# Projections 2 and 3 ahead of the attention, the norm as a column, the rotation from raw projections, positions first

## The chip, the cores and the metric

One core of a Trainium2 chip. The metric is the device time of one execution in microseconds; the lower the better. The engines are called as in the profile: PE (TensorE; PEld is its weight load), DVE (VectorE), ACT (ScalarE), POOL (GpSimd) and SP (SyncE, which issues DMAs here).

## The reference

512 tokens of width 1024 pass through two blocks of two layers each. The change touches the first block alone. One of its layers:

```python
h = _rmsnorm(x, g_pre_mix[l])
z = h @ w_in[l]
zf, zq, zk, zv, zm = jnp.split(z, splits, axis=-1)
y_f = _fourier_mix(zf, w_fourier[l])
q = _rope(zq.reshape(b, s, N_Q_HEADS, HEAD_DIM), positions)
k = _rope(zk.reshape(b, s, N_KV_HEADS, HEAD_DIM), positions)
y_a = _window_attn(q, k, v, sink[l])
mkv = _rmsnorm(mem, g_mem[l]) @ w_mem_kv[l]
km, vm = jnp.split(mkv, 2, axis=-1)
y_m = _memory_attn(zm.reshape(b, s, N_MEM_HEADS, HEAD_DIM), km, vm)
y = jnp.concatenate([_rmsnorm(y_f, ..), _rmsnorm(y_a, ..), _rmsnorm(y_m, ..)], axis=-1) @ w_out[l]
x = x + _rmsnorm(y, g_post_mix[l])
h = _rmsnorm(x, g_pre_ffn[l])
gate, up = jnp.split(h @ w_ffn_in[l], 2, axis=-1)
x = x + _rmsnorm((jax.nn.silu(gate) * up) @ w_ffn_out[l], g_post_ffn[l])
```

`_rmsnorm` multiplies by a gain and by one number per token, 1/sqrt(mean of squares + eps). `_rope` rotates each head by an angle from the token's position, half of the head against the other half. The window attention sees 128 tokens to either side; the memory attention sees 256 memory tokens, the same in both layers.

## The kernel before

Activations lie with the features on the partitions and the 512 tokens along the row, so x is 8 tiles of 128x512. Every product is done to nearly float32 accuracy as three matmuls (`mm3`): each factor is split into a rounded high half and the low half that is left (`split`, `split_gain`), and high x low, low x high and high x high are added up. A weight tile of 256 KB is loaded twice by POOL's DMA queue (`halves`): once as the high half, then ScalarE or VectorE negates that, and a second DMA adds the weight to it, which leaves the low half. A projection of 128 features is 8 x 3 = 24 matmuls.

The gain of a norm is put into the split of x. The factor per token commutes with the projections, so it is multiplied onto them behind PSUM: `enter` (838) makes the halves and the sum of the squares of x, and `late` makes the factor `rb` as a tile of 128x512 by `wide` (817): two matmuls with ones, then mean, square root, reciprocal and one Newton step, all 512 wide. The other form, used elsewhere, is `inv` (801) with `bcast` (856): matmuls against one column of ones put the sums into 4 columns, POOL takes the power -1/2 of 128x4, VectorE multiplies that onto an identity, and one matmul against ones spreads it over the partitions.

A layer of the first block, `block1` (1190), has ten projections of `a_in`: 0 to 3 are the queries (a pair of heads each), 4 the keys, 5 the values, 6 and 7 the memory's queries, 8 and 9 the Fourier branch. Projections 4, 0, 5 and 1 come first: in layer 0 by `open`, which takes the weights as they arrive and waits with the norm, in layer 1 by `linear`, in halves of 256 columns. `ev` (1195) then takes each out of PSUM, times `rb`; for 0 to 4 it rotates (four SP DMAs swap the halves of the heads, times `sin1`, plus the other times `cos1`), and splits. The rotation tables come from `positions` and `trig`, called in `body` (921) behind the loads of x.

Then four pairs of window heads and two pairs of memory heads follow, two pairs ahead: `ask` (scores, softmax), `answer` (transposes), `put` (product with the values). Between these, `pull` takes matmuls from the generator `fillers` (1236), to keep PE busy: projections 2, 3 and 6, in layer 0 the memory's norm and its keys and values (`mem_in`, `mem_k`, `mem_v`; each of the two splits the 8 memory tiles of 128x256 anew), then 7, 8, 9 and the Fourier products. Each `yield` gives a cost in us as the program reckons it: 0.68 for three matmuls of a projection (5.44 for a projection), 0.7 for each of twelve Fourier steps (8.4). In layer 1 the pulls ask for 2 x 5.4 + 12 x 1.3 + 4 x 3.3 = 39.6. The norms of the three groups, the output projection `a_out` and the feed-forward part follow. Layer 1's memory keys and values lie beside layer 0's feed-forward part.

None of this is issued in the order written. `Plan` records every operation; `schedule` (425) then gives each engine its queue: PE's in the order recorded, every other operation by its `need`, the earliest PE time that depends on it by estimated costs, and many of them to the engine that is free. So every instruction of the profile has one line, 646 (649 in the changed kernel), and its names are those of tiles: `s` is one of 100 SBUF tiles of 2 KB per partition, `ps` one of 8 PSUM banks, `in_...` a tensor in memory, `ones`, `onesr`, `ident`, `nhalf` and `cols` constants, `rms` and `rinv` the columns of a norm.

## Time and profile before

| | |
|---|---|
| median of 3 runs | 3483.54 us (3479.14 to 3483.74) |
| profiled execution | 3481.36 us, its span 3479.6 us |
| granted PE clock, mean | 0.992 |
| PE busy | 3404.2 us (98%), 16296 matmuls |
| PEld, DVE, ACT, POOL busy | 2844.1 (82%), 1923.0 (55%), 893.1 (26%), 1748.9 (50%) |
| DMA | 635.93 MB, mean 183 GB/s |
| chain that ended last | PE 90%, DVE 4%, DMA 2%, the rest 4% |

A busy share is that of the whole span. The timeline of an engine lists runs of like instructions with their start, their duration and, in brackets, the idle time ahead of them and what ended it. The table of windows sums, for a stretch of the span, each engine's busy time and its instructions; the granted clock is a share of full speed.

### The profile page before, as it was taken

The numbers are of one execution on the slowest core, as the hardware profiler recorded it, in microseconds if no ns is written. First come the engines' busy times: TensorE is split into PE (matmuls) and PEld (weight loads), VectorE is DVE, ScalarE is ACT, GpSimd is POOL, SyncE is SP. The second block draws the span as 40 slices with busy tenths as digits, with TensorE's granted clock in tenths as the row PEclk, the third lists the DMA queues.
The fourth block names the chain that finished last, engine by engine and source line by source line (L and its number), as shares of the span: only waits on it lengthen the run. The fifth ranks groups of instructions, "written<-read, shape, count | busy, mean of one in ns | idle before, by whom it ended". The sixth has DMA issues, their size and how long they took to land.

```text
span 3479.6 us, 44666 instructions
## 1 busy us (share of the span) xinstructions
PE 3404.2 (98%) x16296; PEld 2844.1 (82%) x16296; DVE 1923.0 (55%) x3916; ACT 893.1 (26%) x1732; POOL 1748.9 (50%) x2433
## 2 busy tenths in 40 slices
PE   6999999899999999999999999999999999999998
PEld 4788888778888988888888888888888888888887
DVE  7964433876432733259997534244423999744332
ACT  5741002543000301016723200010001573411000
POOL 2455464364446544653456544664465336654462
PEclk8999999999999999999999999999999999999999
DMA  6688897798789887985899977998799669998794
GB/s 174 145 186 184 164 207 148 156 193 183 153 169 208 207 181 157 239 212 103 172 197 249 220 152 158 220 204 200 150 225 219 130 130 222 230 239 160 158 202 104
DMA packets 360444, 635.93 MB, mean 183 GB/s; under 512 B 40608, under 2 KB 63904, under 8 KB 360224
## 3 DMA queue, kind: packets, MB, share of 16 engines
q0 software_dynamic: 346752, 612.56, 82.4%
q1 hardware_dynamic: 13472, 20.52, 1.9%
q8 instruction: 128, 2.10, 0.2%
q14 instruction: 92, 0.75, 0.1%
HBM read 624.00 MB, written 6.29 MB: 181 GB/s over the span
## 4 chain that ended last, share of the span: by engine, by line
PE 90%; DVE 4%; DMA 2%; issue 1%; ACT 1%; POOL 1%; SPq 0%; POOLq 0%; DVEq 0%; ACTq 0%
PE ps L646 90%; DVE s L646 4%; ACT s L646 1%; DMA s<-in_x 1%; POOL s L646 0%; DMA s<-in_b_in 0%; DMA s<-in_pos 0%; DMA s<-in_a_in 0%; DMA s<-s 0%; POOL rinv L646 0%; DVE mx L646 0%; DMA s<-in_a_out 0%; DMA s<-in_a_mk 0%; SPq L646 0%; DVE sp L646 0%
## 5 line engine op out<-in xcount | busy, mean ns | idle before, releaser
L646 PE MATMUL ps<-s 128*128 128x512 f32 (+2 forms) x15706 | 3350.9, 376 | 44.6 <-DVE s L646 32.4
L646 PEld LDWEIGHTS ps<-s 128*128 128x128 f32 (+1 forms) x15706 | 2775.6, 188 | 587.9 <-DVE s L646 29.7
L646 POOL DMA_DIRECT2D s<-in_b x1088 | 786.0, 1024 | 666.2 <-DVE s L646 312.2
L646 ACT ACTIVATE s<-s 128x512 fp32r<-128x512 f32 (+2 forms) x702 | 396.9, 601 | 1713.0 <-DVE s L646 1142.4
L646 DVE TENSOR_TENSOR s<-ps,s 128x512 f32<-128x512 f32 (+4 forms) x642 | 397.9, 637 | 580.8 <-PE ps L646 571.6
L646 DVE TENSOR_SCALAR s<-s 128x512 fp32r<-128x512 f32 (+2 forms) x847 | 341.5, 422 | 486.3 <-DMA s<-in_b 283.9
L646 POOL DMA_DIRECT2D s<-in_a_f x544 | 397.4, 1089 | 354.3 <-DVE s L646 199.3
L646 DVE TENSOR_TENSOR s<-s 128x512 f32<-128x512 f32 (+2 forms) x822 | 500.7, 626 | 64.1 <-ACT s L646 36.5
L646 POOL DMA_DIRECT2D s<-in_b_in x368 | 290.4, 1030 | 263.4 <-ACT s L646 84.0
L646 DVE SCALAR_TENSOR_TENSOR s<-s,vecs 128x256 fp32r<-128x256 f32 (+25 forms) x446 | 288.3, 680 | 6.3 <-ACT s L646 3.2
L646 ACT ACTIVATE s<-s,vecs 128x512 f32<-128x512 f32 (+2 forms) x221 | 139.5, 652 | 307.1 <-DVE s L646 294.2
L646 DVE SCALAR_TENSOR_TENSOR s<-ps,s 128x512 f32<-128x512 f32 (+1 forms) x33 | 22.3, 674 | 187.2 <-PE ps L646 187.0
L646 ACT ACT_TABLE_LOAD x68 | 87.2, 1283 | 42.0 <-DVE s L646 40.2
L646 ACT ACTIVATE s<-ps 128x512 f32<-128x512 f32 (+1 forms) x40 | 21.4, 534 | 274.0 <-PE ps L646 251.9
L646 DVE CAST s<-s 128x512 fp32r<-128x512 f32 x192 | 83.8, 436 | 6.5 <-DMA s<-in_pos 1.1
L646 POOL DMA_DIRECT2D s<-in_a_in x64 | 47.2, 931 | 76.2 <-DVE s L646 24.4
L646 DVE RECIPROCAL s<-s 128x128 f32<-128x128 f32 (+1 forms) x46 | 76.5, 1673 | 7.8 <-ACT s L646 7.8
L646 ACT ACTIVATE s<-s,nb 128x256 f32<-128x256 f32 (+3 forms) x128 | 70.6, 553 | 25.9 <-DVE nb L646 25.7
L646 POOL DMA_DIRECT2D s<-in_a_out x64 | 49.5, 1125 | 47.9 <-PE ps L646 30.1
L646 PE MATMUL ps<-ident,s 128*128 128x128 f32 x392 | 56.7, 275 | 14.2 <-DVE s L646 14.2
L646 ACT CAST s<-ps 128x256 fp32r<-128x256 f32 (+4 forms) x142 | 59.9, 455 | 34.0 <-PE ps L646 28.5
L646 POOL TENSOR_TENSOR rinv<-rms,nhalf 128x2 f32<-128x2 f32 (+1 forms) x19 | 20.8, 1165 | 92.4 <-DVE rms L646 91.2
(71 smaller groups left out, 869.6 us busy)
## 6 DMA issues: line engine op xcount, KB each, us to landing
s<-in_b POOLq DMA_DIRECT2D x1024, 256.0 KB, 6.4
s<-in_a_f POOLq DMA_DIRECT2D x512, 256.0 KB, 6.3
s<-in_b_in POOLq DMA_DIRECT2D x368, 256.0 KB, 6.2
s<-in_a_in POOLq DMA_DIRECT2D x64, 256.0 KB, 7.1
s<-in_a_out POOLq DMA_DIRECT2D x64, 256.0 KB, 6.3
s<-in_b_out POOLq DMA_DIRECT2D x64, 256.0 KB, 7.2
s<-in_b POOLq DMA_DIRECT2D x64, 128.0 KB, 6.5
s<-in_b_mo POOLq DMA_DIRECT2D x32, 256.0 KB, 6.0
```

The source lines that it names most:

```text
L646: getattr(getattr(nc, op.eng), op.fn)(*[real(v) for v in op.args], **{k: real(v) for k, v in op.kw.items()})
```

## The change

- The rotation tables get an earlier `need`: `hurry` (30 us for the positions, 18 for the tables) is taken off it in `schedule`.
- `enter` has a parameter `short`. In layer 1 (1) the norm is made by `inv` and `bcast` in place of `wide`. In layer 0 (2) as well, and the 8 squares of x are not added up but all go to `inv`, which is 32 one-column matmuls.
- The rotation starts from the raw projection: `swapped` copies it from PSUM and sends the four swap DMAs; the two tables are multiplied by `rb` once (`turns`), and the projection in PSUM and its swapped copy by these.
- Projections 2 and 3 leave the fillers. In layer 0 they stand behind the first four, ahead of the norm and of all six evictions; in layer 1 they are added to the first group's list, the norm and the evictions again behind all six.
- The memory tiles are no longer multiplied by their norm. The keys of the memory are multiplied by it behind PSUM (`mem_rb`), the values by a column (`mem_r`). In layer 0 the halves are made once for keys and values.

```diff
@@ -388,6 +389,7 @@
         op.lead = self.lead
+        op.hurry = self.hurry
         self.ops.append(op)
@@ -438,6 +440,7 @@
                     op.need = min(op.need, max(p.base for p in op.preds) + self.DRAIN)
+                op.need -= op.hurry
             for p in op.preds:
@@ -835,21 +838,25 @@
-    def enter(self, g, halves=False):
+    def enter(self, g, halves=False, short=0):
...
                 self.split_gain(self.x[k][:, c], self.vec(g, k), [v[:, c] for v in a[k]])
-        for c in HALVES if halves else [ALL]:
+        parts = [s]
+        if short == 2:
+            parts = [self.square(x) for x in self.x]
+        for c in [] if short == 2 else HALVES if halves else [ALL]:
             for k in range(KD):
...
         def late():
-            self.rb = self.wide([s], D)
+            self.rb = self.bcast(self.inv(parts, D))[1] if short else self.wide(parts, D)
@@ -928,8 +935,11 @@
         if self.nl1:
+            nc.hurry = 30.0
             pf = self.positions(0)
+            nc.hurry = 18.0
             self.cos1, self.sin1 = self.trig(0, pf), self.trig(1, pf)
+            nc.hurry = 0.0
         for l in range(self.nl1):
@@ -1189,18 +1199,29 @@
         nc, I = self.nc, self.I
-        a, late = self.enter(f"g_pre{l}", l > 0)
+        a, late = self.enter(f"g_pre{l}", l > 0, 1 if l else 2)
         z = {}
+        turns = {}
+        def swapped(ps):
+            t, b = self.t(), self.t()
+            nc.copy(t, ps)
+            for g in range(4):
+                nc.sync.dma_start(out=b[32 * g:32 * g + 32], in_=t[32 * (g ^ 1):32 * (g ^ 1) + 32])
+            return b
         def ev(m, ps):
-            t = self.tt(ps, self.rb)
             if m < 5:
-                b = self.t()
-                for g in range(4):
-                    nc.sync.dma_start(out=b[32 * g:32 * g + 32], in_=t[32 * (g ^ 1):32 * (g ^ 1) + 32])
-                self.tt(b, self.sin1, out=b)
-                self.tt(t, self.cos1, out=t)
+                b = swapped(ps)
+                if not turns:
+                    for i, c in enumerate((self.cos1, self.sin1)):
+                        turns[i] = self.tt(c, self.rb)
+                t = self.tt(ps, turns[0])
+                self.tt(b, turns[1], out=b)
                 self.tt(t, b, ALU.add, out=t)
+            else:
+                t = self.tt(ps, self.rb)
             if m == 5:
@@ -1215,10 +1236,15 @@
             done = self.open(src(ms), a, lambda i, ps: ev(ms[i], ps))
-            late()
-            done()
+            def both():
+                late()
+                done()
+            self.linear(src([2, 3]), a, lambda i, ps: ev(i + 2, ps), hold=2, before=both)
         else:
-            self.linear(src(ms), a, lambda i, ps: ev(ms[i], ps), hold=4, before=late, first=4)
+            ms += [2, 3]
+            self.linear(src(ms), a, lambda i, ps: ev(ms[i], ps), hold=6, before=late, first=4)
         nsink = self.small(8, "nsink")
@@ -1234,13 +1260,14 @@
         def fillers():
-            rest = [2, 3, 6]
+            rest = [6]
             yield from self.steps(src(rest), a, lambda i, ps: ev(rest[i], ps))
...
                 yield 0.0
-                yield from self.mem_k(0)
-                yield from self.mem_v(0)
+                both = self.mem_split(0)
+                yield from self.mem_k(0, both)
+                yield from self.mem_v(0, both)
             last = [7, 8, 9]
@@ -1350,9 +1377,8 @@
         nc.vector.tensor_copy(out=self.mem_r, in_=r)
-        rb = self.bcast(self.mem_r, n=2)[1]
-        for k in range(KD):
-            self.tt(self.mem[k], rb, out=self.mem[k])
+        self.mem_rb = self.fixed("mem_rb", [128, NMEM])
+        nc.copy(self.mem_rb, self.bcast(self.mem_r, n=2)[0])
@@ -1368,8 +1394,8 @@
-    def mem_k(self, l):
-        hs, ls = self.mem_split(l)
+    def mem_k(self, l, split=None):
+        hs, ls = split or self.mem_split(l)
         self.km = []
@@ -1378,11 +1404,11 @@
             h, l_ = self.t(F32R)[:, :NMEM], self.t(F32R)[:, :NMEM]
-            self.split(ps, h, l_)
+            self.split(self.tt(ps, self.mem_rb), h, l_)
             self.km.append((h, l_))
-    def mem_v(self, l):
-        hs, ls = self.mem_split(l)
+    def mem_v(self, l, split=None):
+        hs, ls = split or self.mem_split(l)
         w = [self.wload(self.I[f"a_mv{l}"][i]) for i in range(2)]
@@ -1392,7 +1418,9 @@
                 yield 0.36
-            self.split(ps, vh[:, NMEM * j:NMEM * j + NMEM], vl[:, NMEM * j:NMEM * j + NMEM])
+            t = self.t()[:, :NMEM]
+            self.nc.scale(t, ps, self.mem_r[:, j:j + 1])
+            self.split(t, vh[:, NMEM * j:NMEM * j + NMEM], vl[:, NMEM * j:NMEM * j + NMEM])
         self.vm = ([vh[:, NMEM * j:NMEM * j + NMEM] for j in range(2)],
```

First place: DVE at the program's start. `s<-s,first` are the low halves of x, `s<-s,cols` belong to the rotation tables. Before:

```order
L646 MEMSET ones 128x128
L646 MEMSET nhalf 128x4
L646 CAST onesr<-ones 128x128
L646 MEMSET s 128x512 x2
L646 TENSOR_SCALAR s<-s 128x512
L646 TENSOR_SCALAR s<-s,first 128x512
L646 SCALAR_TENSOR_TENSOR s<-s,first 128x512
L646 TENSOR_TENSOR s<-s 128x512
L646 SCALAR_TENSOR_TENSOR s<-s,first 128x512 x3
```

With the change:

```order
L649 MEMSET ones 128x128
L649 MEMSET nhalf 128x4
L649 CAST onesr<-ones 128x128
L649 TENSOR_SCALAR s<-s 128x512
L649 CAST s<-s 128x512
L649 TENSOR_SCALAR s<-s,cols 128x512 x4
L649 TENSOR_SCALAR s<-s 128x512 x2
L649 SCALAR_TENSOR_TENSOR s<-s 128x512 x6
L649 TENSOR_SCALAR s<-s,cols 128x512 x2
L649 SCALAR_TENSOR_TENSOR s<-s,first 128x512
L649 TENSOR_TENSOR s<-s 128x512
```

The cast of the positions and fourteen operations on the two tables now stand ahead of the first low half of x.

Second place: PE at the program's start, from the first projections into the first pair's scores (`64*128`-row matmuls of 256 and 384 columns, `ps<-s`). Before:

```order
L646 MATMUL ps<-s 128x512 x96
L646 MATMUL ps<-s,onesr 128x512 x2
L646 MATMUL ps<-ident,s 128x128 x4
L646 MATMUL ps<-s 128x256 x2
L646 MATMUL ps<-s 128x384 x3
```

With the change:

```order
L649 MATMUL ps<-s 128x512 x144
L649 MATMUL ps<-ones,s 128x1 x32
L649 MATMUL ps<-s,ones 128x512
L649 MATMUL ps<-ident,s 128x128 x4
L649 MATMUL ps<-s 128x256 x2
L649 MATMUL ps<-s 128x384 x4
```

48 matmuls (projections 2 and 3) moved ahead of the norm, and the two matmuls of the wide norm gave way to 32 of one column and the spreading one.

Third place: POOL's queue at the head of layer 1, from the last load of the memory's weights (`in_a_mv`) on. Before:

```order
L646 DMA s<-in_a_mv 128x512
L646 DMA s<-in_a_in 128x512 x29
L646 DMA s<-in_a_out 128x512 x2
L646 DMA s<-in_a_in 128x512 x3
L646 DMA s<-in_a_out 128x512 x5
L646 DMA s<-in_a_in 128x512 x6
L646 DMA s<-in_a_out 128x512 x16
```

With the change:

```order
L649 DMA s<-in_a_mv 128x512
L649 DMA s<-in_a_in 128x512 x29
L649 DMA s<-in_a_out 128x512 x2
L649 DMA s<-in_a_in 128x512 x3
L649 DMA s<-in_a_out 128x512 x4
L649 DMA s<-in_a_in 128x512 x2
L649 DMA s<-in_a_out 128x512 x3
L649 DMA s<-in_a_in 128x512 x4
L649 TENSOR_TENSOR rinv<-rms,nhalf 128x4
L649 DMA s<-in_a_out 128x512 x7
```

The power of the layer's norm (`rinv<-rms,nhalf`) is new in this queue, with 47 loads between it and the last of the memory's weights.

## Rows read from the trace of the kernel before

**Rows 1.** Timeline of PE, opening: start us, us, instructions, [idle before, ended by].

```profile
8.20 4.52 PE L646 MATMUL ps<-s 128*128 128x512 f32 x9 [8.20 <-DVE s L646]
12.91 20.59 PE L646 MATMUL ps<-s 128*128 128x512 f32 x87 [0.19 <-ACT s L646]
...
58.30 17.30 PE L646 MATMUL ps<-s 64*128 64x256 f32 x96 [7.39 <-DVE s L646]
```

**Rows 2.** Timeline of PE, head of layer 1.

```profile
621.19 0.63 PE L646 MATMUL ps<-s,onesr 128*128 128x512 f32 x2
...
631.48 0.60 PE L646 MATMUL ps<-ident,s 128*128 128x128 f32 x4
644.87 16.98 PE L646 MATMUL ps<-s 64*128 64x256 f32 x96 [12.79 <-DVE s L646]
```

**Rows 3.** Timeline of DVE, head of layer 1.

```profile
629.34 1.89 DVE L646 TENSOR_TENSOR s<-ps,s 128x512 f32<-128x512 f32 x3
...
639.22 2.02 DVE L646 TENSOR_TENSOR s<-s 128x512 f32<-128x512 f32 x3 [5.74 <-DMA s<-s]
```

**Rows 4.** Windows, first scores to output projection, layers 0 and 1: window, length, busy times.

```profile
core 0: us, PE busy (x) PEld busy (x) DVE busy (x) ACT busy (x) POOL busy (x), PEclk, DMA share, GB/s
58.30:174.20 115.90, 107.80 (x722) 91.83 (x723) 105.26 (x299) 86.35 (x234) 40.64 (x59) 0.97 0.58 124
644.87:740.90 96.03, 92.97 (x604) 78.09 (x605) 87.01 (x250) 67.74 (x189) 39.85 (x59) 0.96 0.63 132
```

**Rows 5.** Timeline of DVE, opening.

```profile
6.44 0.43 DVE L646 TENSOR_SCALAR s<-s 128x512 fp32r<-128x512 f32 x1 [4.09 <-DMA s<-in_a_in]
...
29.57 0.43 DVE L646 CAST s<-s 128x512 f32<-128x512 int32 x1 [1.05 <-DMA s<-in_pos]
...
30.52 0.48 DVE L646 TENSOR_SCALAR s<-s,cols 128x512 f32<-128x512 f32 x1
30.92 0.68 DVE L646 TENSOR_TENSOR s<-s 128x512 f32<-128x512 f32 x1
...
33.45 0.68 DVE L646 SCALAR_TENSOR_TENSOR s<-s 128x512 f32<-128x512 f32 x1
34.05 0.68 DVE L646 TENSOR_TENSOR s<-s 128x512 f32<-128x512 f32 x1
```

**Rows 6.** Windows, a stretch in which TensorE is busy throughout.

```profile
20.00:30.00 10.00, 10.00 (x45) 7.94 (x44) 5.97 (x10) 7.12 (x13) 1.82 (x3) 1.00 1.18 367
```

**Rows 7.** Timeline of PE: matmuls of one column, and those that spread a norm.

```profile
179.37 1.84 PE L646 MATMUL ps<-ones,s 128*128 128x1 f32 x16
181.07 3.02 PE L646 MATMUL ps<-s 128*128 128x512 f32 x12
...
732.90 1.10 PE L646 MATMUL ps<-s,ones 128*128 128x512 f32 x2 [0.57 <-DVE s L646]
```

**Rows 8.** Timeline of POOL ahead of and in layer 1.

```profile
597.03 0.82 POOL L646 TENSOR_TENSOR rinv<-rms,nhalf 128x2 f32<-128x2 f32 x1 [5.14 <-DVE rms L646]
...
635.47 0.87 POOL L646 DMA_DIRECT2D s<-in_a_in  x1 [0.98 <-DMA s<-in_a_in]
...
639.11 0.85 POOL L646 DMA_DIRECT2D s<-in_a_in  x1 [0.92 <-DMA s<-in_a_in]
```

**Rows 9.** Timeline of ACT at the first scores.

```profile
62.72 1.34 ACT L646 ACTIVATE s<-s 128x256 f32<-128x256 f32 x4
```

**Rows 10.** Groups by form, DVE, 58.3 to 174.2: count, busy us, mean ns, idle before.

```profile
L646 DVE TENSOR_TENSOR s<-s 128x512 f32<-128x512 f32 x17 | 11.4, 688 | 0.9 <-ACT s L646 0.8
L646 DVE SCALAR_TENSOR_TENSOR s<-s,vecs 128x256 fp32r<-128x256 f32 x20 | 8.9, 481 | 0.0
...
L646 DVE TENSOR_TENSOR s<-s 128x256 f32<-128x256 f32 x15 | 6.2, 422 | 0.2
```

**Rows 11.** The same view, 644.87 to 740.9.

```profile
L646 DVE TENSOR_TENSOR s<-s 128x512 f32<-128x512 f32 x16 | 10.6, 686 | 0.1
```

**Rows 12.** Windows, end of layer 1's attention.

```profile
710.00:740.90 30.90, 28.86 (x192) 24.09 (x191) 25.51 (x55) 17.85 (x43) 23.38 (x37) 0.94 1.09 246
```

More of the change, by code (lines that the diff above doesn't have):

```diff
@@ L302 @@
     __slots__ = ("ways", "eng", "fn", "args", "kw", "index", "preds", "succs", "tiles", "cost", "table", "need",
-                 "wait", "end", "ready", "lead", "base")
+                 "wait", "end", "ready", "lead", "base", "hurry")
 class Engine:
@@ L326, in __init__ @@
         self.lead = self.AHEAD
+        self.hurry = 0.0
         for e in self.ENGINES:
```

## Prediction

> **What bounds the kernel now.** I read the stage table first, then TensorE's timeline at the head of each layer of the first block, then the engines that it waits for there. TensorE is the bound of the program as a whole, so only its idle time can be won, and it lies in few places. In the opening [rows 1] it starts at 8.20 us, runs 96 matmuls until 33.5, and then has almost nothing until the first scores at 58.30: about 23 us idle. In layer 1 the four early projections end at 631.5 and the first scores start at 644.87, 12.8 us idle [rows 2]; there VectorE waits 5.74 us for the swap transfers of the rotation [rows 3]. After the first scores things change: from there to the output projection, VectorE is busy 105.26 of 115.90 us in layer 0 and 87.01 of 96.03 in layer 1, TensorE 107.80 and 92.97 [rows 4]. Both engines are nearly full there, so taking work from TensorE alone saves less than that work.
>
> A difference under 0.2% (7.0 us) can't be told from none here. The profiled execution took 3481.36 us, 2.2 under the median 3483.54; the sum is made against 3481.36.
>
> **Layer 0, the opening.** (1) VectorE now does the rotation tables first. Its first instruction, a negation, still waits for the same load and starts at 6.44 [rows 5]. Behind it come one cast, eight TENSOR_SCALARs and six SCALAR_TENSOR_TENSORs, and only then the low half of x that the first matmul needs (order, first place). The same operations in the trace: 0.43 for the cast, 0.40 and 0.60 from one start to the next for the others [rows 5]: 0.43 + 8 x 0.40 + 6 x 0.60 = 7.2 us. So the first matmul moves from 8.20 to 15.4. (2) Of this much comes back. Before, 96 matmuls took 25.3 us, being fed as the loads came in; well fed, TensorE does 45 in 10 us, 0.222 each [rows 6], so 96 take 21.3. I add 1.0 (estimate) because the first twelve need four low halves that VectorE makes one by one. End: 37.7 instead of 33.5. The load of positions ahead of x shifts x by 256 KB at 367 GB/s [rows 6], 0.7 us; the 7.2 us on VectorE hide it. (3) Projections 2 and 3: 48 x 0.222 = 10.7, end 48.4. Their corrected low weights are issued from POOL in the same place as before, while TensorE still works on the first 96, so no wait is added. (4) The norm in columns: eight squares x four one-column matmuls = 32, each 1.70 / 16 = 0.106 (from the start of the sixteen to the start of what follows [rows 7]), 3.4 us, end 51.8. It replaces two matmuls, seven additions on VectorE and the square-root chain. (5) Then a chain in which nothing overlaps: 0.4 for mean and hand-over, 0.82 for POOL's power [rows 8], 0.68 for the diagonal product (as a product of two tiles [rows 5]), 1.10 for the spreading matmul [rows 7], 0.3 for hand-overs: 3.3, so the copy out of PSUM starts at 55.1. (6) Up to the scores VectorE has twelve 512-wide operations in order (copy, two tables times norm, then k, v and q0), 12 x 0.60 = 7.2; ScalarE's cast of q0 (0.6), which stands behind six squares of the memory at 0.335 [rows 9], some 0.8 late; 0.7 for hand-overs: 9.3. **First scores at 64.4 instead of 58.30: 6.1 later, with 10.7 us of projections already done.** The swaps cost nothing, as raw projections are copied out and sent while projections 2 and 3 run; without that cover the wait of [rows 3] is back.
>
> **Layer 0, from the scores to the output projection.** VectorE loses four rotation products (4 x 0.67), eight products of memory and norm (8 x 0.41) and the second split of the memory (8 x 0.445), and gains two products with the norm (2 x 0.41) [rows 10]: 2.7 + 3.3 + 3.6 - 0.8 = 8.8. The scaling of v lies on ScalarE or VectorE, four small operations per layer, outside any wait. With VectorE at its share of before the stage takes 96.5 x 115.90 / 105.26 = 106.2, or 9.7 less; with TensorE at its share, 97.1 x 115.90 / 107.80 = 104.4, or 11.5 less. I take the first, since VectorE had the longest unbroken stretches. **Layer 0: 6.1 - 9.7 = -3.6.**
>
> **Layer 1.** There the norm's matmuls stand behind projections 2 and 3, where before the two of the wide norm were done at 621.19, in the middle of the four projections [rows 2]. So the norm comes at 630.9 (without those two) + 10.7 + 0.4 = 642.0, while before it was already spread by 629.3. And it now takes POOL's power, in POOL's queue, behind the weight loads. Up to the last load that left before the gap, at 639.11, POOL issues 42 loads after the last of the memory's weights; ahead of the power there are now 47 (order, third place), five more. Each takes 0.85 to issue and, when it has to wait for earlier ones to land, 1.82 (from 635.47 to 639.11 in two steps [rows 8]). So the last ends between 639.11 + 6 x 0.85 = 644.2 and 639.11 + 5 x 1.82 + 0.85 = 649.1, while the mean is ready at 642.4. I take 645.5, near the lower end, because seven of the last thirteen are plain loads without an addition; lateness 3.1, bounds 1.8 and 6.7. [...]
>
> Then 0.82 + 0.68 + 1.10 + 0.3 gives the copy at 648.4, and 9.3 less the 0.8 of the squares, 8.5, **the first scores at 656.9 instead of 644.87: 12.0 later, again with 10.7 us done ahead.** Behind it VectorE loses four rotation products (4 x 0.66 [rows 11]): 84.4 x 96.03 / 87.01 = 93.1, 2.9 less. By TensorE's share it would be 82.3 x 96.03 / 92.97 = 85.0, 11.0 less. **Layer 1: 12.0 - 2.9 = +9.1.**
>
> The second block is untouched, and so is the work between. The two later products for the memory of layer 1 lie beside the feed-forward matmuls. **Sum: -3.6 + 9.1 = +5.5, 3486.9 us; I write 3487.** That is 0.1% over the median: no change that can be told, on the slow side.
>
> [...]
>
> **Rivals.** A, faster: TensorE stays the bound after the scores, so the 10.7 us are saved whole in both layers, and the power doesn't wait. Then layer 0 gives 6.1 - 11.5 = -5.4, layer 1 gives 12.0 - 3.1 - 11.0 = -2.1, together -7.5: 3474. For it: TensorE's share is 93% and 97%. Against it: VectorE's 91% in both, and TensorE's waits there end on VectorE. Chance 0.20.
>
> B, slower: the fillers run out in layer 1. In the kernel's own units they hold 4 projections x 5.44 + 8.4 = 30.2 instead of 41.0, and the pulls ask for 39.6. So from the fourth pair on, scores, transposes and products of the memory heads stand bare, each waiting for the last. The nearest row for a tail in latency is the end of this stage, where VectorE is busy 25.51 of 30.90 us, 0.826 [rows 12]. At that share the stage takes 84.4 / 0.826 = 102.2, 6.2 more than before instead of 2.9 less: +14.6 in all, 3496. It decides when TensorE's idle time in that stage passes 14 us (3.1 before, 10.8 in my sum). For it: the last pairs need few matmuls and long chains. Against it: VectorE has less to do there in the end. Chance 0.30.
>
> C, in between: the sum as above, within bounds of a few us. Chance 0.50; of this some 0.40 is within 0.2%, 0.08 beyond it on the slow side, 0.02 on the fast.
>
> **Numbers.** The sum gives 3487. The low end is A at 3474, cut to 3475; the high end takes the power at its late bound (+3.6), layer 1's stage with nothing saved (+2.9) and half the saving of layer 0 (+4.8): 3498. Faster 0.20 (A but for its weakest part, and C's 0.02), same 0.42, slower 0.38 (B and C's 0.08).
>
> **What would show it.** First matmul near 15.4 and 96 done by 38; scores near 64 and 657; in layer 1 the power at 645 or later with POOL's loads right ahead of it; TensorE's idle time after the scores larger than 8.1 and 3.1 us, ended by VectorE. Wrong if the first matmul starts below 11 us, if layer 1's scores start before 652, or if the stages shrink by over 10 us each.

## The result, and the profile after

The changed kernel takes 3510.98 us, the median of 4 runs (3509.95 to 3514.09), against 3483.64 before: 27.3 us slower, ratio 1.0082 with a 95% interval of 1.0066 to 1.0098. The forecast was 3487, at most 3498. The profiled execution is the slowest of the four (3514.09, span 3512.3) and that of before lies 2.3 under its median (3481.36), so the traces differ by 32.7.

Four marks on TensorE cut the span: the first scores of layer 0, the first one-column norm behind layer 0's feed-forward part, the first scores of layer 1, the wide norm that opens the second block. (The expectations below call the second mark "layer 1's first memory norm" and "layer 0's last norm"; it is the latter.)

| us | before | after | difference | forecast |
|---|---|---|---|---|
| start to first scores, layer 0 | 58.30 | 75.44 | +17.1 | +6.1 |
| to layer 0's last norm | 528.17 | 525.33 | -2.8 | -9.7 |
| to first scores, layer 1 | 58.40 | 72.00 | +13.6 | +12.0 |
| to the second block | 170.29 | 173.31 | +3.0 | -2.9 |
| second block | 2664.4 | 2666.2 | +1.8 | 0 |

Nearly all of it lies ahead of the scores, and what was to be won behind them is small in layer 0 and a loss in layer 1. TensorE's timeline of the changed kernel, opening (it answers to [rows 1]; start us, us, instructions, idle time before and what ended it):

```profile
14.66 0.76 PE L649 MATMUL ps<-s 128*128 128x512 f32 x1 [14.66 <-DVE s L649]
16.65 0.80 PE L649 MATMUL ps<-s 128*128 128x512 f32 x1 [1.22 <-ACT s L649]
18.22 35.38 PE L649 MATMUL ps<-s 128*128 128x512 f32 x142 [0.78 <-ACT s L649]
53.44 9.13 PE L649 MATMUL ps<-ones,s 128*128 128x1 f32 x64
64.67 2.08 PE L649 MATMUL ps<-s,ones 128*128 128x512 f32 x2 [2.10 <-DVE s L649]
70.11 1.09 PE L649 MATMUL ps<-ident,s 128*128 128x128 f32 x4 [3.36 <-issue]
75.44 3.56 PE L649 MATMUL ps<-s 64*128 64x256 f32 x24 [4.25 <-ACT s L649]
80.31 7.44 PE L649 MATMUL ps<-s 128*128 128x512 f32 x43 [1.31 <-DVE mx L649]
94.96 1.01 PE L649 MATMUL ps<-s 64*128 64x256 f32 x5 [7.20 <-DVE s L649]
```

The 32 one-column matmuls are 64 records, two for each (passes, below). Before the change TensorE went on for 17.30 us from the first scores [rows 1]; now 24 matmuls of the first pair and 43 more (projection 6 and 19 of the second pair's) are followed by 7.20 us idle. The two stretches of the column matmuls, in the table of windows (PE busy and records, granted clock, DMA share, GB/s):

```profile
53.44:58.00 4.56, 4.56 (x43) 1.00 1.01 309
58.00:62.57 4.57, 4.57 (x24) 0.54 0.49 131
```

TensorE is busy throughout, but the granted clock falls from 1.00 to 0.50 near the middle (0.50 throughout from 58.50 to 62.57), and a pass goes from 0.11 to 0.19 us. The same view, five microseconds each, for the pace of the first matmuls; first the changed kernel:

```profile
15.00:20.00 5.00, 3.00 (x6) 1.00 1.16 380
20.00:25.00 5.00, 5.00 (x14) 1.00 1.16 381
25.00:30.00 5.00, 5.00 (x24) 1.00 0.84 248
```

and the kernel before:

```profile
10.00:15.00 5.00, 4.81 (x14) 1.00 1.14 333
15.00:20.00 5.00, 5.00 (x24) 1.00 1.16 382
```

A busy stretch can hold 14 matmuls or 24, and the full pace begins near 25 us instead of 15, although the first matmul is only 6.5 later. The groups by form (count, busy us, mean ns, idle before) tell why: matmuls of the same shape at 18.22 to 24.06 and at 24.4 to 30 us, then those of a later run (layer 1's memory as fillers, told of below) at 64.4 to 70 us:

```profile
L649 PE MATMUL ps<-s 128*128 128x512 f32 x14 | 6.3, 642 | 0.8 <-ACT s L649 0.8
L649 PE MATMUL ps<-s 128*128 128x512 f32 x26 | 6.2, 395 | 0.0
L649 PE MATMUL ps<-s 128*128 128x512 f32 x13 | 5.9, 638 | 3.3 <-DVE mx L649 3.3
```

The last ran at a granted clock of 0.50, as their window says:

```profile
65.00:70.00 5.00, 5.00 (x13) 0.50 0.00 0
```

So the first matmuls of the program take about as long as those at 0.50, in the kernel before until about 13.4 us (ten matmuls in 5.2 us, 685 ns on the mean, and 403 from there to 20 us) and in the changed kernel until 24.06, though the table gives 1.00 for them. The head of layer 1, TensorE (it answers to [rows 2]):

```profile
620.63 32.96 PE L649 MATMUL ps<-s 128*128 128x256 f32 x227 [2.10 <-DMA s<-in_a_in]
653.44 0.72 PE L649 MATMUL ps<-ones,s 128*128 128x1 f32 x6
654.02 2.76 PE L649 MATMUL ps<-s 128*128 128x512 f32 x11
656.62 0.28 PE L649 MATMUL ps<-ones,s 128*128 128x1 f32 x2
662.49 2.08 PE L649 MATMUL ps<-s,ones 128*128 128x512 f32 x2 [5.59 <-DVE s L649]
667.97 1.09 PE L649 MATMUL ps<-ident,s 128*128 128x128 f32 x4 [3.40 <-DVE s L649]
672.77 3.70 PE L649 MATMUL ps<-s 64*128 64x256 f32 x24 [3.72 <-ACT s L649]
```

and POOL's, where the power comes right behind the last of four loads (it answers to [rows 8]):

```profile
659.79 0.86 POOL L649 DMA_DIRECT2D s<-in_a_in  x1 [0.82 <-DMA s<-in_a_in]
660.35 1.36 POOL L649 TENSOR_TENSOR rinv<-rms,nhalf 128x4 f32<-128x4 f32 x1
```

The windows of layer 1 from its scores to the middle of the output projection (PE, PEld, DVE, ACT, POOL busy, granted clock, DMA share, GB/s); the changed kernel:

```profile
672.77:784.58 111.81, 99.98 (x612) 81.59 (x613) 94.66 (x267) 70.05 (x193) 49.78 (x72) 0.92 0.62 129
```

and the same stretch of the kernel before:

```profile
644.87:753.18 108.31, 104.42 (x659) 86.86 (x659) 95.13 (x268) 73.45 (x199) 50.50 (x74) 0.97 0.68 147
```

There are 47 matmuls fewer on record, and the stretch is 3.5 us longer. The 10.7 us that left it are taken by more idle time (11.8 instead of 3.9) and by a lower granted clock (0.92 instead of 0.97), at which 47 matmuls fewer keep TensorE busy for only 4.4 us less.

### The profile page after: what moved, and what is told of

It is laid out like the page before. It is cut to its first block, busy times and chain, and to the rows that moved or that the text cites. A ratio compares the mean times of both kernels' runs of the same rounds, so it can differ in the third digit from the quotient of the medians.

```text
span 3512.3 us, 44762 instructions
## 1 busy us (share of the span) xinstructions
PE 3428.8 (98%) x16368; PEld 2866.5 (82%) x16368; DVE 1904.3 (54%) x3904; ACT 881.6 (25%) x1711; POOL 1752.5 (50%) x2435
## 4 chain that ended last, share of the span: by engine, by line
PE 75%; DVE 3%; issue 1%; DMA 1%; POOL 1%; ACT 0%; POOLq 0%; DVEq 0%; ACTq 0%
PE ps L649 75%; DVE s L649 3%; DMA s<-in_b_in 1%; POOL s L649 1%; ACT s L649 0%; POOL rinv L649 0%; DVE mx L649 0%; DVE sp L649 0%; DVE nb L649 0%; POOLq L1760 0%; DVE rc L649 0%; DVEq L649 0%; DVEq L1760 0%; DVE rms L649 0%; POOLq L649 0%
## 5 line engine op out<-in xcount | busy, mean ns | idle before, releaser
L649 PE MATMUL ps<-s 128*128 128x512 f32 (+3 forms) x15706 | 3357.7, 377 | 51.3 <-DVE s L649 29.6
L649 PEld LDWEIGHTS ps<-s 128*128 128x128 f32 (+2 forms) x15706 | 2783.7, 188 | 595.1 <-issue 24.9
L649 ACT ACTIVATE s<-s 128x512 fp32r<-128x512 f32 (+3 forms) x682 | 384.9, 600 | 1697.0 <-DVE s L649 1128.3
L649 DVE TENSOR_TENSOR s<-ps,s 128x512 f32<-128x512 f32 (+5 forms) x634 | 393.8, 638 | 592.6 <-PE ps L649 587.1
L649 DVE TENSOR_TENSOR s<-s 128x512 f32<-128x512 f32 (+3 forms) x801 | 485.2, 623 | 54.9 <-ACT s L649 34.1
L649 DVE SCALAR_TENSOR_TENSOR s<-s,vecs 128x256 fp32r<-128x256 f32 (+22 forms) x438 | 284.2, 683 | 6.6 <-ACT s L649 3.6
L649 ACT ACTIVATE s<-ps 128x512 f32<-128x512 f32 (+1 forms) x40 | 21.3, 533 | 273.4 <-PE ps L649 235.5
L649 DVE CAST s<-s 128x512 fp32r<-128x512 f32 (+2 forms) x184 | 79.2, 430 | 5.1
L649 PE MATMUL ps<-ident,s 128*128 128x128 f32 x392 | 59.9, 287 | 11.3 <-ACT s L649 4.5
L649 PEld LDWEIGHTS ps<-ident,s 128*128 128x128 f32 x392 | 48.9, 148 | 23.8 <-issue 11.1
```

Of the source, the lines that this page charges most:

```text
L649: getattr(getattr(nc, op.eng), op.fn)(*[real(v) for v in op.args], **{k: real(v) for k, v in op.kw.items()})
```

## The experiments

The theory at first: every part of the head costs by itself (tables ahead of x, 64 passes of columns, projections ahead), and in layer 1 nothing pays the projections back. All medians are of runs beside the kernel before on the same chip. It took 3481.95 beside the first four runs below and 3483.61 to 3483.71 beside the others, so a difference between runs of different groups is good to about 2 us.

### Layer 0's head: tables and columns

Without the earlier `need`:

```diff
-            nc.hurry = 30.0
+            nc.hurry = 0.0
-            nc.hurry = 18.0
+            nc.hurry = 0.0
```

> The changed kernel without the earlier need of positions and rotation tables; all else as changed. Theory (the opening lost 17.1 us by itself: 6.5 because VectorE makes the tables ahead of the first low half, some 5 because TensorE is then fed slowly, some 6 because the 32 one-column matmuls run as 64 passes of 0.143 us): the first matmul goes back to 8.2, projections 4, 0, 5, 1, 2, 3 end near 46 instead of 53.6, first scores near 67 instead of 75.4, the whole 3503 (8 less than 3511). Rival 1 (loads, not VectorE, set when TensorE can work): the first matmul is early but the last of the 144 still ends at 52 to 54, scores at 74 to 76, the whole 3509 to 3512. Rival 2 (the tables now are what the rotation waits for): scores at 72 to 76 with VectorE making tables after the norm.

Measured: 3497.76 (3495.00 to 3500.14), 13.2 less than the changed kernel. TensorE's timeline:

```profile
7.49 1.22 PE L649 MATMUL ps<-s 128*128 128x512 f32 x2 [0.88 <-DVE s L649]
...
46.95 5.79 PE L649 MATMUL ps<-ones,s 128*128 128x1 f32 x38
...
65.43 3.57 PE L649 MATMUL ps<-s 64*128 64x256 f32 x24 [4.01 <-ACT s L649]
```

The first matmul of a projection is back at 7.5 and the scores come 10.0 earlier, more than the 8 expected: some of the column passes now run between other matmuls, 38 are left for the end. Both rivals fall. The stretch behind is 1.7 shorter, and layer 1's head and the second block give 1.0 and 1.2 more, about what the untouched second block differs by between two traces (1.8 in the table above).

One sum of squares in layer 0:

```diff
-        a, late = self.enter(f"g_pre{l}", l > 0, 1 if l else 2)
+        a, late = self.enter(f"g_pre{l}", l > 0, 1 if l else 1)
```

> The changed kernel with layer 0's squares added up first, as in layer 1: 4 one-column matmuls (8 passes) in place of 32 (64 passes). Theory: 56 passes x 0.143 = 8.0 us go from a stretch in which nothing else can run, VectorE has 27 us idle there for the seven additions; first scores near 67.5 instead of 75.4, the whole 3503. Rival (the columns stand beside the wait for loads of projections 2 and 3, or the additions are late): scores not before 73, the whole 3509 to 3512.

Measured: 3498.06 (3494.90 to 3501.41), 12.9 less.

```profile
53.38 0.95 PE L649 MATMUL ps<-ones,s 128*128 128x1 f32 x8
56.43 1.12 PE L649 MATMUL ps<-s,ones 128*128 128x512 f32 x2 [2.10 <-DVE s L649]
60.80 1.09 PE L649 MATMUL ps<-ident,s 128*128 128x128 f32 x4 [3.25 <-issue]
68.29 3.68 PE L649 MATMUL ps<-s 64*128 64x256 f32 x24 [6.41 <-DVE s L649]
```

Eight passes take 0.95, so 0.12 each instead of 0.14, and the spreading product 1.12 instead of 2.08: in the changed kernel the granted clock is 0.50 there (64.67 to 66.75). The scores come 7.2 earlier (8.0 expected), and the stretch to layer 0's last norm is 520.16 instead of 525.33, which I had not expected. In the changed kernel VectorE makes the memory's sums and halves between 78.5 and 90.4, among its work for the first softmax; here between 56.3 and 72.5, ahead of it. That this is the cause of the 5 us is argued from the order, not tried by itself.

### One layer as before

Layer 1 with the wide norm and with projections 2 and 3 as fillers:

```diff
-            ms += [2, 3]
-            self.linear(src(ms), a, lambda i, ps: ev(ms[i], ps), hold=6, before=late, first=4)
+            self.linear(src(ms), a, lambda i, ps: ev(ms[i], ps), hold=4, before=late, first=4)
...
-            rest = [6]
+            rest = [2, 3, 6] if l else [6]
...
-        a, late = self.enter(f"g_pre{l}", l > 0, 1 if l else 2)
+        a, late = self.enter(f"g_pre{l}", l > 0, 0 if l else 2)
```

> Layer 0 as changed; in layer 1 projections 2 and 3 are fillers again and the norm is the wide one (rotation from raw projections and the later memory norm stay). Theory (layer 1 lost 13.6 us up to its first scores, by 10.7 of projections ahead, and 3.5 behind them, for lack of fillers): both come back, layer 1's first scores near 72 us after its first memory norm as early as 58 to 60 us after it, the whole 3511 - 17 = 3494. Rival 1 (only the wait for POOL's power costs, 4.7 us; the projections are paid back later): 3504 to 3507. Rival 2 (the raw rotation costs as well, since the swaps no longer hide): 3498 to 3502, with VectorE waiting over 4 us for the swap transfers in layer 1.

Measured: 3493.09 (3490.91 to 3495.75), 17.9 less, as the theory had it. Layer 1's head is 51.83, even 6.6 less than before the change: the raw rotation does cover the swaps there. But from the scores to the second block it takes 173.60, 3.3 more than before.

Layer 0 as before, layer 1 as changed:

```diff
-            nc.hurry = 30.0
+            nc.hurry = 0.0
-            nc.hurry = 18.0
+            nc.hurry = 0.0
...
-        a, late = self.enter(f"g_pre{l}", l > 0, 1 if l else 2)
+        a, late = self.enter(f"g_pre{l}", l > 0, 1 if l else 0)
...
-            def both():
-                late()
-                done()
-
-            self.linear(src([2, 3]), a, lambda i, ps: ev(i + 2, ps), hold=2, before=both)
+            late()
+            done()
...
-            rest = [6]
+            rest = [6] if l else [2, 3, 6]
```

> Layer 1 as changed; in layer 0 the tables come behind x, the norm is the wide one and projections 2 and 3 are fillers again (rotation from raw projections and the later memory norm stay). Theory: layer 0's 14.3 us come back and the smaller work on VectorE helps a little more: first scores near 58, the whole 3494 to 3497. Rival (the loss of layer 0 lies in the raw rotation or the memory norm): first scores after 62 or a stage from there longer than before, the whole 3500 or more.

Measured: 3497.18 (3493.66 to 3498.53), 13.8 less, just over the theory's range. Scores at 56.16, layer 0's last norm at 586.74 (586.47 before). Layer 0 gains nothing by the smaller work on VectorE. The two losses add up: measured over the kernel before on the same chip, putting back layer 1 takes away 16.2 of the 27.3 and layer 0 12.1, together 28.3, and both at once (the next run) 28.5.

### What is left of the change when its losses are taken out

Rotation and memory norm alone; the edits of the run before this one, and layer 1's of the one before that:

```diff
-        a, late = self.enter(f"g_pre{l}", l > 0, 1 if l else 2)
+        a, late = self.enter(f"g_pre{l}", l > 0, 0 if l else 0)
...
-            rest = [6]
+            rest = [2, 3, 6]
```

> Only the rotation from raw projections and the later memory norm; tables, norms, and projections 2 and 3 as in the kernel before, in both layers. Theory from the two runs that put one layer back: layer 0 as long as before (+0.3), layer 1 3.3 shorter: 3478 to 3480. Rival (the work taken off VectorE counts after the scores, by its share): 8 to 12 less, 3470 to 3474.

Measured: 3482.43 (3477.53 to 3484.85), ratio 0.9993 (0.9984 to 1.0002): no difference, 2.4 above the theory's range. Layer 1's head is 7.3 shorter (51.10) and its stage 6.6 longer (176.91): what the head gains, the stage loses. It is the same in layer 0, where the scores come 3.4 earlier and the stretch to its last norm is 4.1 longer (532.22). The windows of layer 0 from its scores to the middle of the output projection, the kernel before and then this run:

```profile
58.30:187.03 128.73, 119.33 (x776) 100.57 (x777) 112.17 (x316) 89.08 (x239) 52.22 (x75) 0.98 0.62 132
54.95:188.00 133.05, 120.90 (x777) 102.08 (x777) 112.47 (x319) 81.21 (x217) 54.18 (x78) 0.96 0.61 128
```

VectorE is busy 112.47 us in it against 112.17: its work behind the scores hasn't become less, since evictions that the earlier scores leave behind take the place of what was saved (this last is argued). The rival, that work off VectorE counts by VectorE's share, falls.

The early projections in layer 0 alone, with tables behind x and one sum of squares (`hurry` 0; layer 1's `linear` and `rest` as in the run with layer 1 as before):

```diff
-        a, late = self.enter(f"g_pre{l}", l > 0, 1 if l else 2)
+        a, late = self.enter(f"g_pre{l}", l > 0, 0 if l else 1)
```

> Projections 2 and 3 ahead in layer 0 alone, with the tables behind x (as in the run without the earlier need) and one sum of squares (as in the run with one sum); layer 1 with its fillers and the wide norm as before; rotation from raw projections and the later memory norm in both. Theory (the two losses in layer 0's head are separate, and early projections cost nothing there without them): first scores 59 to 62, layer 1's first memory norm near 580 (586.5 in the kernel before), layer 1 some 3 us shorter than before as in the run with layer 1 as before; the whole 3472 to 3476, under the kernel before. Rival (the two gains of 13 overlap, since either way the 144 matmuls wait for loads): memory norm at 585 to 588, the whole 3478 to 3482.

Measured: 3471.44 (3469.53 to 3476.10), ratio 0.9966 (0.9954 to 0.9979): **12 us faster than the kernel before**, the lowest median of all. TensorE's timeline:

```profile
42.21 2.76 PE L649 MATMUL ps<-s 128*128 128x512 f32 x11
44.82 0.28 PE L649 MATMUL ps<-ones,s 128*128 128x1 f32 x2
47.36 1.12 PE L649 MATMUL ps<-s,ones 128*128 128x512 f32 x2 [2.27 <-DVE s L649]
51.87 1.09 PE L649 MATMUL ps<-ident,s 128*128 128x128 f32 x4 [3.39 <-issue]
56.68 3.86 PE L649 MATMUL ps<-s 64*128 64x256 f32 x24 [3.72 <-ACT s L649]
63.87 9.85 PE L649 MATMUL ps<-s 128*128 128x512 f32 x43 [3.33 <-DVE mx L649]
```

The first scores start 1.6 earlier than before the change with two projections more behind them, and layer 0's last norm stands at 577.71, 8.8 earlier. Against the run before this one, which keeps projections 2 and 3 as fillers, the scores are 1.7 later and the stretch to the last norm is 11.2 shorter (521.03): there the 10.7 us come back whole. So in layer 0 the idea holds, together with the column norm of one sum (the two were not tried apart); the early tables and the 32 columns spoilt it.

The same with the rotation behind the norm, as in the kernel before:

```diff
...
+            t = self.tt(ps, self.rb)
...
-                b = swapped(ps)
...
+                b = self.t()
+                for g in range(4):
+                    nc.sync.dma_start(out=b[32 * g:32 * g + 32], in_=t[32 * (g ^ 1):32 * (g ^ 1) + 32])
+                self.tt(b, self.sin1, out=b)
+                self.tt(t, self.cos1, out=t)
...
-            else:
-                t = self.tt(ps, self.rb)
```

> The mended version with the rotation after the norm, as in the kernel before. Theory: the swaps again stand bare in both layers; heads some 6 longer (layer 0's scores at 62 or later, layer 1's head 57 to 59 instead of 51.8), of which the stages give back some 4, since the raw rotation only moves VectorE's work behind the scores; the whole 3474 to 3479. Rival (the raw rotation is worth its whole 6 per layer): 3482 to 3485.

Measured: 3479.20 (3476.18 to 3483.14), 7.8 more, just over the theory's range. Scores at 60.79, layer 0's last norm at 583.27, layer 1's head 59.07 and its stage 171.46 (56.68, 577.71, 51.84 and 174.65 with the raw rotation). So by the traces it is worth 5.6 up to layer 0's last norm and 4.0 in layer 1. About 1 us of the 5.6 is the spreading product, which takes 2.08 here and 1.12 with the raw rotation:

```profile
47.54 2.08 PE L649 MATMUL ps<-s,ones 128*128 128x512 f32 x2 [2.50 <-DVE s L649]
```

In layer 0 the raw rotation with the memory norm was worth nothing without the early projections (last norm at 587.17 against 586.47); with them it is. In layer 1 no run of this pair has early projections, and there the same exchange gave 0.7 by itself (head and stage together 228.0 instead of 228.7), so its 4.0 is no firm number.

### Layer 1: the power, the columns, the fillers

The changed kernel with the wide norm in layer 1:

```diff
-        a, late = self.enter(f"g_pre{l}", l > 0, 1 if l else 2)
+        a, late = self.enter(f"g_pre{l}", l > 0, 0 if l else 2)
```

> The changed kernel, but layer 1's norm is the wide one again; projections 2 and 3 stay ahead there. Theory (layer 1 loses by the 10.7 us of projections ahead that nothing pays back, and the power's wait of 4.7 is only what the column chain has over the wide one's 8): layer 1's head 1 to 4 us shorter than 72.0, the whole 3507 to 3510. Rival (the wait for POOL behind the loads is most of the loss in layer 1): the head 8 or more shorter, the whole 3500 to 3503.

Measured: 3507.48 (3506.62 to 3509.23), 3.5 less; head 68.07 instead of 72.00. The power behind the loads costs, but it is the small part.

The changed kernel with columns in layer 1, and projections 2 and 3 as fillers there:

```diff
-            ms += [2, 3]
-            self.linear(src(ms), a, lambda i, ps: ev(ms[i], ps), hold=6, before=late, first=4)
+            self.linear(src(ms), a, lambda i, ps: ev(ms[i], ps), hold=4, before=late, first=4)
...
-            rest = [6]
+            rest = [2, 3, 6] if l else [6]
```

> The changed kernel, but in layer 1 projections 2 and 3 are fillers again; the norm stays in columns. Theory: the power now stands ahead of the loads of the output projection and isn't late; head of layer 1 51 to 54 as with the wide norm, the whole 3492 to 3496 (3493 with the wide norm). Rival (the power is late here too, by over 4 us): head 56 or more, the whole 3497 to 3500.

Measured: 3498.24 (3496.38 to 3502.33): the theory falls and the rival stands. POOL's timeline:

```profile
641.01 0.87 POOL L649 DMA_DIRECT2D s<-in_a_in  x1 [1.10 <-DMA s<-in_a_in]
642.14 1.73 POOL L649 DMA_DIRECT2D s<-in_a_in  x2 [0.26 <-DMA s<-in_a_in]
643.25 1.68 POOL L649 TENSOR_TENSOR rinv<-rms,nhalf 128x4 f32<-128x4 f32 x1
```

The mean is ready at 639.2 and the power starts 4.0 later, though only loads of projections stand ahead of it; then the spreading product stands in TensorE's order behind all four projections (648.77). Head 56.39 against 51.83 with the wide norm, stage 177.75 against 173.60.

Projections 2 and 3 ahead in layer 1 as well, but behind the norm and the evictions of the first four, added to the mended version:

```diff
+            ms += [2, 3]
             self.linear(src(ms), a, lambda i, ps: ev(ms[i], ps), hold=4, before=late, first=4)
```

> The mended version (layer 0 mended) with projections 2 and 3 ahead in layer 1 too, but behind the norm and the evictions of the first four, which they now cover; wide norm. Theory (layer 1 has too few fillers left, so what is done ahead there is paid and not won back): the cover shortens the head against the run with the wide norm (68.1 from layer 0's last norm to the scores) to about 60, still 8 more than the 51.8 without early projections; the stage from the scores to the second block stays at 172 to 175; the whole 3477 to 3481. Rival (it was only the bare norm chain): the head at 56 to 60, and the stage 8 to 10 shorter, 164 to 167; the whole 3468 to 3472.

Measured: 3484.15 (3481.28 to 3488.23), 12.7 more than the mended version and 3 over the range. Head 62.93, 11.1 longer, and the stage 174.23, only 0.4 shorter: 48 matmuls (10.7 us) moved, and all of them paid for. The rival falls.

Then the same with more fillers: layer 1's memory keys and values, 96 matmuls, go into its attention; and the control, in which the mended version gets this edit alone.

```diff
+            else:
+                both = self.mem_split(l)
+                yield from self.mem_k(l, both)
+                yield from self.mem_v(l, both)
...
-                pull(3.3 if l else 5.3)
+                pull(5.3)
...
-            for _ in self.mem_k(l + 1):
-                pass
...
-            for _ in self.mem_v(l + 1):
-                pass
```

> The run before this one, and layer 1's memory keys and values (96 matmuls, about 11 us) are no longer made beside layer 0's feed-forward part but are fillers in layer 1's attention. Theory (fillers run out there): the 11 us go out of the stretches before and find TensorE idle in the stage, which grows by 0 to 4 only; the whole 7 to 11 less than the run before this one, 3468 to 3472. Rival (the stage is set by VectorE, whatever TensorE has to do): the stage grows by 9 or more, the whole within 3 of the run before this one.

> Control: the mended version (no early projections in layer 1) with layer 1's memory keys and values as fillers in its attention. Theory: there were enough fillers already, so the stage grows by about the 11 us that it takes in, and the whole stays within 3 of the mended version's 3471. Rival (any more filler helps): 6 or more less than 3471.

| median us | projections 2, 3 of layer 1 as fillers | ahead |
|---|---|---|
| memory of layer 1 beside the feed-forward part | 3471.44 | 3484.15 |
| memory of layer 1 as fillers | 3477.52 | 3472.96 |

With few fillers the early projections cost 12.7; with the memory's matmuls in the attention they gain 4.6 (3472.96, 1 over the range, and no better than 3471.44 without either). Most of this turn is not the fillers' doing, though, as the stretches show:

| us | projections 2, 3 as fillers | ahead |
|---|---|---|
| layer 1's head, memory beside the feed-forward part | 51.84 | 62.93 |
| layer 1's head, memory as fillers | 49.36 | 50.59 |
| scores to the second block, memory beside | 174.65 | 174.23 |
| scores to the second block, memory as fillers | 185.99 | 181.38 |

The plan does not hold TensorE strictly to the order recorded: where the operands of a matmul aren't ready by its estimates, `schedule` takes a later one that is. So in the mended version the two matmuls of layer 1's norm stand ahead of the last 82 of the first four projections, which cover the norm's chain. In the control they stand behind all four, and TensorE is idle for 10.72 us, which early projections can fill. TensorE behind the norm in the mended version, in the control and with both edits:

```profile
612.69 9.99 PE L649 MATMUL ps<-s 128*128 128x256 f32 x82
623.58 0.66 PE L649 MATMUL ps<-ident,s 128*128 128x128 f32 x4 [0.90 <-DVE s L649]
616.90 1.11 PE L649 MATMUL ps<-ident,s 128*128 128x128 f32 x4 [10.72 <-DVE s L649]
607.13 11.04 PE L649 MATMUL ps<-s 128*128 128x512 f32 x48
618.42 0.65 PE L649 MATMUL ps<-ident,s 128*128 128x128 f32 x4 [0.25 <-DVE s L649]
```

The early projections therefore cost 11.1 in the one head and 1.2 in the other. In the stage their leaving gives back 0.4 with few fillers and 4.6 with the memory's. By the traces they cost 11.5 in the first row of the table of medians and gain 2.3 in the second; of these 13.8 us, 9.9 lie in the head and only 4.2 in the stage, and only the latter speak for the fillers. The windows from the scores to the output projection; first the run with early projections and few fillers:

```profile
641.34:754.00 112.66, 99.96 (x611) 82.09 (x612) 93.46 (x265) 69.47 (x193) 49.73 (x72) 0.92 0.65 133
```

and with the memory as fillers:

```profile
624.88:745.00 120.12, 113.00 (x709) 95.16 (x709) 95.43 (x272) 73.75 (x202) 58.78 (x85) 0.91 0.74 159
```

TensorE's idle time there goes from 12.7 to 7.1 us while 98 more matmuls are on record. The stage up to the second block grows by 7.2 (174.23 to 181.38), in the control by 11.3 (174.65 to 185.99). I had expected 0 to 4, so only a part of the 11 us found idle time; and the control, expected within 3 of 3471, came out 6 over. The direction is the theory's, its sizes are not. The control's stage pays 11.3 for the memory's matmuls, while the stretches ahead of it give back only 7.3: 4.9 up to layer 0's last norm and 2.5 in layer 1's head, where the norm's chain now stands bare. The other 2 us lie in the opening and the second block.

## Why the prediction was wrong, step by step

**Right.** The first matmul at 14.66 (15.4 forecast); the copy to the scores 8.65 (9.3); projections 2 and 3 10.5 (10.7: the raw copy of the last early projection starts at 42.99 and the columns at 53.44). In layer 1, counted from layer 0's last norm, the mean was forecast for 656.7 and came at 656.93, the power for 659.8 and came at 660.35, the scores for 671.2 and came at 672.77. The swaps were indeed covered. The 3.1 us of lateness in the sum rest on POOL taking its queue in the listed order, which no run shows by itself. The power at 660.35 agrees with it: it comes right behind the loads, 3.4 us after the mean. The gaps of [rows 8] were weaker support: two end on a load, but the power's own there ends on VectorE. The sum's hand-overs (0.3 to 0.7 us a step) stand on no row; from the last column of layer 0 to the spreading product it had 1.9 us, and TensorE's idle time there was 2.10.

**"32, each 1.70 / 16 = 0.106, 3.4 us"**: mis-sized, 9.13. The 16 of [rows 7] were 16 passes of 8 instructions, but I counted 32 instructions from the order and priced each as one pass; 64 x 0.107 would be 6.8. The other 2.3 come with the granted clock, which was 1.00 over the first 43 passes (4.56 us, the row's 0.106 each) and 0.54 on the mean behind them.

**"Well fed, TensorE does 45 in 10 us, so 96 take 21.3. I add 1.0"**: failed. They took 28.3, from 14.66 to 42.99. The step read the 25.3 us of [rows 1] as slow feeding alone. But the first matmuls are slow in both kernels, 642 ns on the mean here and 685 before, as at a granted clock of 0.50 (638): here fifteen took 9.4 us, to 24.06, 2.0 of them idle, where the forecast's pace asks for 3.3, and the other 81 took 18.9, nearly that pace. This is nearly all of the 6.0 that the step lacks, of layer 0's 11.0 in excess. The two waits at the start end with ScalarE's casts at 15.97 and 17.55 us, and ScalarE waits there for weight tiles. Its cast of the second tile, here and then in the kernel before:

```profile
15.97 0.62 ACT L649 CAST s<-s 128x512 fp32r<-128x512 f32 x1 [1.08 <-DMA s<-in_a_in]
12.23 0.62 ACT L646 CAST s<-s 128x512 fp32r<-128x512 f32 x1 [0.62 <-DMA s<-in_a_in]
```

It starts 3.7 us later, now that the loads of the positions and of `cols` stand ahead of x; the prediction had 0.7 for that, hidden. Whether these waits also made the slow pace last longer isn't shown.

**"With VectorE at its share of before the stage takes 106.2"**: failed. It forecast 2.9 less in layer 1 and 3.0 more came; in layer 0 it forecast 9.7 less, and 2.8 less came. That 8.0 less came there with one sum of squares and 7.1 less in the mended version looks like the forecast, but by luck: with the rotation and the memory norm alone, which were to take 8.8 us off VectorE behind the scores, VectorE was as busy as before and the stretch 4.1 longer. In the mended version it is the projections' leaving that makes it shorter, by 11.2 against that run. This is what rival A said of layer 0 (-11.5); it had 0.20 for both layers together. A busy share is no law of a stage. In layer 1 the raw rotation lengthens the stage (173.60 to 176.91 in the three runs with it, the wide norm and projections 2 and 3 as fillers; 170.29 before), and the projections' leaving gives back 0.4 and 0.6 in the two pairs of runs that differ by it alone.

**Rival B** named a want of fillers in layer 1, 30.2 us of them for pulls of 39.6, and priced it at +14.6 for the whole. Its number for layer 1 is near, 18.2 against 16.6, but not by its sum: it had the stage 6.2 longer for want of fillers, and the 3.0 that came are there without early projections as well. What the want of fillers can explain is that 10.7 us moved out of the stage gave back 0.4; the test with the memory's matmuls supports it for the 4.2 us above, and the rest is open. For the whole it was too cheap because it stood on layer 0's wrong -3.6. I gave it 0.30 and took the share argument as likelier, though the count of the fillers spoke against it.

**Layer 1's head** was called nearly right (+12.0, measured +13.6), and I took it for a price that the stage would pay back. It is the largest single loss: of 17.3 us in layer 1 (243.9 from layer 0's last norm to the second block, the mean of the four runs with both parts, against 226.6, the mean of the three without either), the early projections with the wide norm make 14.4 and, with the norm between, 10.5, which is their whole working time. There was little for them to fill: with the raw rotation TensorE is idle in that head for 0.9 us behind the first four projections and 5.3 ahead of the scores, and with the projections moved still for 0.7 and 5.8.

## What to carry to other kernels

Moving work of the bound engine ahead of a stage pays in two places: where that engine stands idle ahead of the stage and the work fills the gap, and where the stage has other work to put in its place. Look at both before moving it: in layer 0 here both were there, in layer 1 little of either. Count the filler work that remains against what the stage asks for, and don't scale a stage by busy shares. In a test of two edits against each other, cut the times at the same marks, as a schedule can change elsewhere. Make the engines' first instructions those that the bound engine waits for; tables that are needed 40 us later can wait. Count matmuls in the trace's records, not in the program's instructions, when a row prices them, and note the clock at which the row was taken.

## What the runs showed of the hardware that I had not expected

The granted clock fell within long rows of one-column float32 matmuls. Over 9.13 us of them, busy without a gap, the granted clock was 1.00 in the first half and 0.54 in the second, and a pass went from 0.11 to 0.19 us; the four runs with 64 passes in a row took 9.11 to 10.33 us for them. In the run with tables later, 38 such passes in a row had a mean clock of 0.72. A spreading product took 2.08 us at a granted clock of 0.50 (changed kernel, 64.67) and 1.10 at 1.00 (kernel before, 732.90). In the openings with eight passes it took 1.12 or 1.13 five times (2.10 to 2.68 us idle before it), but 2.08 once (2.50 idle).

TensorE began the program slowly: in the changed kernel 128x512 matmuls up to 24.06 us last 642 ns on the mean, like those at a granted clock of 0.50 (638), and 395 from 24.4 us on, though the table of windows gives 1.00 for both stretches.
